# An MLP's seven products with their weight sums made by transfers: two sums leave VectorE for adding DMAs, and three results are summed in DRAM

## The chip, the cores and the metric

The kernel runs on one core of a Trainium2 chip. The metric is the device time of one execution in microseconds, lower is better. Engines are named as the profile names them: PE multiplies matrices, DVE (VectorE) adds and subtracts, ACT (ScalarE) copies and applies functions, POOL (GpSimd) and SP here mainly issue transfers (DMAs), each from a queue of its own that keeps its order.

## The reference, cut to what matters

One inference step of one layer on 384 tokens: 128 of a prompt and 256 of a sample. A projection feeds two mixers (an mLSTM and a pooling mixer), their output is added to the input, and an MLP with 8192 hidden channels follows. Only the MLP is touched by the change:

```python
    h = _rmsnorm(x, norm_w[2]) * (1 + scale_f) + shift_f
    y = jnp.square(jax.nn.relu(h @ w1)) @ w2      # (384 x 2048) @ (2048 x 8192), then @ (8192 x 2048)
    x = x + gate_f * _rmsnorm(y, norm_w[3])
```

All data are float32. The kernel multiplies in a reduced float32 format, with each operand split into a high part (a rounded copy) and a low part (what is left), and three matmuls (high x high, high x low, low x high) for one product.

## The kernel before

The MLP goes by chunks of 1024 hidden channels, that is 8 tiles of 128: `ch` 0 to 7. Hidden tiles are made by groups of w1 (`w1_group`: four slabs of 24 matmuls of 128x384, with the w1 slab loaded by SP, its high part made on ACT at L134 and its low part on DVE at L135). The second product, with w2, is added up over chunks in `y[0..2]`, one tile of 128 tokens by 2048 columns for each token group.

Chunk 0 multiplies by w2 in the plain way. In chunks 1 to 6 (`S_FIRST` to `S_LAST`), for each of the four blocks `n` of 512 columns, and in chunk 7 for n=0 and 1 (`N_LAST` = 2), `mlp_seven` is used: 26 calls, named (ch, n) here. It takes token groups 1 and 2 and even and odd hidden tiles as a 2x2 of blocks, a 2x2 of w2 (row parity r, column half c) as the other, and forms the product with seven block products instead of eight, by sums of blocks. Token group 0 takes its plain products with the same weights on the way. The hidden side of the sums (s1, s2, s4) is made in `evac_pair`, which takes the hidden tiles out of PSUM. The weight side is made here:

- SP loads four blocks of 512 KB: b11 = (0,0), b21 = (1,0), b22 = (1,1), b12 = (0,1). Tiles come from two pools, tag `raw` (3 buffers, shared with the w1 slabs) and tag `raw2` (2 buffers, b21 and b12).
- DVE forms, each into the place of one operand, T1 = b12 - b11 (L1225), T3 = b22 - b12 (L1231), T2 = b22 - T1 (L1235) and T4 = b21 - T2 (L1239).
- Each of the seven weights b11, b21, b22, T1, T3, T2, T4 is split: high part on ACT (L1189), low part on DVE (L1190). The profile calls them hi_b and lo_b for b11, b21 and b22, hi_t and lo_t for the sums.
- PE runs 11 products of 12 matmuls of 128x256 (L1203 to L1205) into five PSUM banks: `x7`, `yz`, `16`, `23`, `45`. The order of use is b11 and b21, then b22, T1, T3, T2, T4.
- The results: DVE adds the bank halves that belong to one output to `y`. R7 (right half of x7) and R1, R6 (bank 16) belong to several outputs; they are summed over the chunks in two SBUF tiles, r7 and r16 (ACT copies in chunk 1, DVE adds at L1212 later). `seven_done` combines them with `y` once, for n=2 and 3 at the end of chunk 6 and for n=0 and 1 in chunk 7 beside its plain products.

The order of the instructions on each engine and in each queue is set when the kernel is built; each engine runs its own in that order. Within a chunk PE runs seven n=0, seven n=1, one w1 group, seven n=2, seven n=3, three w1 groups. So n=1 follows n=0 directly and n=3 follows n=2; with (7,0) and (7,1) these are 13 pairs back to back, in which the second seven's weights must be loaded and summed while the first runs.

Of the kernel before, what the change touches and what calls it, by code (L numbers as in the profile page):

```python
# [43 lines left out]
def hymba_kernel(  # L44
# [1128 lines left out]
    def mlp_seven(ch, n, strp, r16, r7, feeds=()):  # L1173
# [4 lines left out]
        for m, (r, c) in enumerate(((0, 0), (1, 0), (1, 1), (0, 1))):  # L1178
            pool, tag = ((wp, "raw"), (strp, "raw2"))[m % 2]
            raws[r, c] = pool.tile([P, 1024], F32, tag=tag, name=f"w2_{ch}_{n}_{r}{c}", bufs=3 - m % 2)  # L1180
            nc.sync.dma_start(raws[r, c].rearrange("p (j q) -> p j q", q=256),
                              w2v[:, k0 + r:k0 + 8:2, c0 + 256 * c:c0 + 256 * c + 256])
# [42 lines left out]
        tt(b11, b12, b11, op=ALU.subtract)  # L1225
# [1 line left out]
        tt(yx, banks["x7"][:, 0:256].unsqueeze(1).to_broadcast([P, 2, 256]), yx, op=ALU.add)
# [3 lines left out]
        tt(b12, b22, b12, op=ALU.subtract)  # L1231
# [12 lines left out]
        product("45", 0, 1, 2, w)  # L1244
        if first:
            nc.scalar.activation(r7[:, n], banks["x7"][:, 256:], AF.Copy)
            nc.scalar.activation(r16[:, n], banks["16"], AF.Copy)
# [4 lines left out]

    def seven_done(n, r16, r7):

        tt = nc.vector.tensor_tensor
# [8 lines left out]
        tt(y2, y2, v.unsqueeze(1).to_broadcast([P, 2, 256]), op=ALU.add)
# [105 lines left out]
```

## Time and profile before

| | |
|---|---|
| three runs | 1688.34, 1690.98, 1690.77 us (median 1690.77) |
| span of the profiled execution | 1686.4 us |
| PE busy | 1657.3 us (98%), 10965 matmuls |
| DVE busy | 1341.7 us (80%) |
| ACT busy | 752.3 us (45%) |
| POOL busy | 130.9 us (8%) |
| transfers | 320.95 MB, mean 190 GB/s |
| transfers from POOL (software queue q0) | 13.69 MB |

The profiled execution's own time is shown only as its span, from its first to its last instruction; the runs' times, taken without the profiler, contain what lies around it too, and their median is 4.4 us above this span. PE is nearly always busy, at a granted clock near full speed. A line of the profile's groups gives line, engine, operation, tiles and shapes, count, then busy time in us, mean in ns and idle time before; a line of a timeline gives start and length in us. The buffers' numbers are left out of its names, so raw and raw2 tiles of w2 are both `w` there, and the banks are `y_x` (x7), `y_yz` and `y` (the other three).

### The profile page before, as it was taken

To read this page: it belongs to the slowest core of one execution; us is meant where nothing else is said; L and a number is where in the kernel's file an instruction comes from. 1 tells how busy PE (TensorE), PEld (TensorE's weight loads), DVE (VectorE), ACT (ScalarE), POOL (GpSimd) and SP (SyncE) were. 2 spreads that over 40 slices of the span, in tenths; PEclk is the share of its full clock that TensorE was granted. 3 is DMA by queue.
4 is the path that set the end of the run, shared out by engine and by line. 5 is a ranking of instruction groups with operands and counts; after the bars stand their busy time and mean duration, and the time that the engine had idled before them with its cause. 6 is when DMAs were issued, how large, how long until landed. Compare 5 with 4: busy or idle time off the path is not lost.

```text
span 1686.4 us, 27861 instructions
## 1 busy us (share of the span) xinstructions
PE 1657.3 (98%) x10965; PEld 1583.9 (94%) x10965; DVE 1341.7 (80%) x2009; ACT 752.3 (45%) x1225; POOL 130.9 (8%) x181
## 2 busy tenths in 40 slices
PE   6999999999999999999999999999999999999997
PEld 3888999999999989988999999999999999999996
DVE  3677769898998959997797688988588588588688
ACT  4432355555443345543444444444444444444443
POOL 0000002221000023530000000000000000000120
PEclk9999999999999999999999999999999999999999
DMA  9999858776789964754556245544344443443653
GB/s 305 324 297 304 276 153 256 245 248 221 236 265 308 312 206 126 218 153 137 157 169 195 87 138 178 155 150 142 109 150 127 124 139 113 149 125 111 185 184 134
DMA packets 258195, 320.95 MB, mean 190 GB/s; under 512 B 14752, under 2 KB 223248, under 8 KB 257680
## 3 DMA queue, kind: packets, MB, share of 16 engines
q1 hardware_dynamic: 250256, 303.41, 57.1%
q0 software_dynamic: 5856, 13.69, 2.8%
q10 hardware_dynamic: 1952, 2.07, 0.4%
q8 instruction: 86, 1.41, 0.3%
q14 instruction: 45, 0.37, 0.1%
HBM read 308.61 MB, written 10.51 MB: 189 GB/s over the span
## 4 chain that ended last, share of the span: by engine, by line
PE 83%; DVE 9%; DMA 3%; issue 2%; SPq 1%; ACT 1%; POOL 0%; DVEq 0%; ACTq 0%; POOLq 0%
PE acc_w L144 9%; PE acc_w L143 9%; PE acc_w L145 9%; PE v L476 4%; PE y L1204 4%; PE y L1203 4%; PE y L1205 4%; PE u L476 4%; PE acc_wo L143 3%; PE acc_wo L144 3%; PE acc_wo L145 3%; PE y_yz L1203 2%; PE y_yz L1205 2%; PE y_yz L1204 2%; DVE ada_acc L316 2%
## 5 line engine op out<-in xcount | busy, mean ns | idle before, releaser
L144 PE MATMUL acc_w<-h2l,hi_w 128*128 128x384 f32 (+1 forms) x1024 | 346.2, 338 | 0.5 <-DVE h2l L997 0.5
L143 PE MATMUL acc_w<-h2h,hi_w 128*128 128x384 f32 (+1 forms) x1024 | 344.2, 338 | 1.4 <-ACT h2h L993 1.2
L145 PE MATMUL acc_w<-h2h,lo_w 128*128 128x384 f32 (+1 forms) x1024 | 345.1, 337 | 0.0
L135 DVE TENSOR_TENSOR lo_w<-raw_w,hi_w 128x1024 fp32r<-128x1024 f32 x152 | 185.5, 1222 | 134.2 <-ACT hi_w L134 133.7
L134 ACT ACTIVATE hi_w<-raw_w 128x1024 fp32r<-128x1024 f32 x152 | 160.7, 1058 | 211.8 <-PE acc_w L144 95.2
L316 DVE SCALAR_TENSOR_TENSOR ada_acc<-ada_raw,sg,ada_acc 128x1024 f32<-128x1024 f32 (+1 forms) x240 | 252.1, 1082 | 1.9 <-DMA ada_raw<-in_ada_w_dram 1.9
L143 PEld LDWEIGHTS acc_w<-h2h,hi_w 128*128 128x128 f32 x1024 | 192.2, 188 | 3.1 <-ACT h2h L993 2.0
L144 PEld LDWEIGHTS acc_w<-h2l,hi_w 128*128 128x128 f32 x1024 | 192.5, 188 | 1.2 <-DVE h2l L997 0.8
L145 PEld LDWEIGHTS acc_w<-h2h,lo_w 128*128 128x128 f32 x1024 | 192.4, 188 | 0.3 <-DVE lo_w L135 0.2
L1189 ACT ACTIVATE hi_t<-w 128x1024 fp32r<-128x1024 f32 x104 | 109.6, 1060 | 118.6 <-DVE w L1225 33.6
L1190 DVE TENSOR_TENSOR lo_t<-w,hi_t 128x1024 fp32r<-128x1024 f32 x104 | 126.4, 1221 | 15.1 <-ACT hi_t L1189 14.7
L1190 DVE TENSOR_TENSOR lo_b<-w,hi_b 128x1024 fp32r<-128x1024 f32 x78 | 95.3, 1222 | 40.5 <-ACT hi_b L1189 40.4
L1189 ACT ACTIVATE hi_b<-w 128x1024 fp32r<-128x1024 f32 x78 | 82.6, 1060 | 99.2 <-PE acc_w L144 65.9
L134 ACT ACTIVATE hi_wo<-raw_wo 128x1024 fp32r<-128x1024 f32 x32 | 34.0, 1064 | 83.5 <-DMA raw_wo<-in_w_out_dram 65.7
L923 ACT ACTIVATE z<-acc_w 128x384 f32<-128x384 f32 x54 | 26.3, 487 | 75.0 <-PE acc_w L145 75.0
L476 PE MATMUL v<-hi_v,hh 128*128 128x384 f32 (+1 forms) x144 | 47.8, 332 | 0.0
L476 PE MATMUL v<-lo_v,hh 128*128 128x384 f32 (+1 forms) x144 | 46.6, 324 | 0.0
L476 PE MATMUL v<-hi_v,hl 128*128 128x384 f32 (+1 forms) x144 | 46.5, 323 | 0.0
L134 ACT ACTIVATE hi_v<-raw_v 128x768 fp32r<-128x768 f32 (+1 forms) x24 | 18.9, 795 | 60.8 <-DMA raw_v<-in_w_in_dram 40.9
L135 DVE TENSOR_TENSOR lo_wo<-raw_wo,hi_wo 128x1024 fp32r<-128x1024 f32 x32 | 38.8, 1216 | 8.3 <-ACT hi_wo L134 7.5
L143 PE MATMUL acc_k<-hh,hi_k 128*128 128x384 f32 x128 | 44.2, 345 | 0.0
L143 PE MATMUL acc_o<-hh,hi_o 128*128 128x384 f32 x128 | 43.9, 343 | 0.0
(2264 smaller groups left out, 4552.8 us busy)
## 6 DMA issues: line engine op xcount, KB each, us to landing
raw_w<-in_w_dram SPq DMA_DIRECT2D x152, 512.0 KB, 4.3
ada_raw<-in_ada_w_dram SPq DMA_DIRECT2D x130, 512.0 KB, 5.1
w<-in_w_dram SPq DMA_DIRECT2D x104, 512.0 KB, 4.2
raw_wo<-in_w_out_dram SPq DMA_DIRECT2D x32, 512.0 KB, 5.2
u<-in_ada_w_dram SPq DMA_DIRECT2D x18, 512.0 KB, 6.1
raw_u<-in_w_in_dram SPq DMA_DIRECT2D x16, 512.0 KB, 7.1
raw_q<-in_w_in_dram SPq DMA_DIRECT2D x16, 512.0 KB, 4.6
raw_k<-in_w_in_dram SPq DMA_DIRECT2D x16, 512.0 KB, 4.9
```

The lines of the kernel that those rows point to most:

```text
L134: nc.scalar.activation(hi[:, 0:n], raw[:, 0:n], AF.Copy)
L135: low = lambda: nc.vector.tensor_tensor(lo[:, 0:n], raw[:, 0:n], hi[:, 0:n].bitcast(F32), op=ALU.subtract)
L143: nc.tensor.matmul(ps, lh, rh, start=start, stop=False)
L144: nc.tensor.matmul(ps, lh, rl, start=False, stop=False)
L145: mm3.ins = nc.tensor.matmul(ps, ll, rh, start=False, stop=stop).ins
L316: nc.vector.scalar_tensor_tensor(acc[:, g, :], raw[:, a, :], cj, acc[:, g, :], op0=ALU.mult, op1=ALU.add)
L476: nc.tensor.matmul(acc[i][:, 0:n], h[k0 + k][a][:, i * P:(i + 1) * P], (hi, lo)[b][:, k, :], start=k == 0 and a + b == 0, stop=k == nk - 1 ...
L1189: nc.scalar.activation(hi, raw, AF.Copy)
L1190: nc.vector.tensor_tensor(lo, raw, hi.bitcast(F32), op=ALU.subtract)
L1203: nc.tensor.matmul(acc, xh, wh, start=start and j == 0, stop=False)
L1204: nc.tensor.matmul(acc, xh, wl, start=False, stop=False)
L1205: nc.tensor.matmul(acc, xl, wh, start=False, stop=stop and j == 3)
```

## The change

T1 and T3 are no longer made by DVE. Their tile is loaded by SP with block (0,1), and then POOL issues an adding transfer of block (0,0) or (1,1) from DRAM onto it. [...] A seven has five loads and two adding transfers of 512 KB in place of four loads, and b12 has no tile of its own. The tag raw2 has three buffers.

R7, R1 and R6 are no longer summed in SBUF. ACT copies the three into a tile `stage` (128x768, 2 buffers), and POOL stores it to DRAM (`r_dram[n]`) in chunk 1 and adds it there later, 384 KB each. `seven_done` loads the sums back with a POOL transfer. The tiles r7 and r16 (12 KB a partition) are gone.

```diff
--- before.py
+++ after.py
@@ -929,7 +929,7 @@
         a11, a21, a12, a22 = z0[:, P:2 * P], z0[:, 2 * P:], z[:, P:2 * P], z[:, 2 * P:]
         s1, s2, s4 = (s[:, i * P:(i + 1) * P] for i in range(3))
         tt = nc.vector.tensor_tensor
-        tt(s1, a21, a22, op=ALU.add)
+        tt(s1, a21, a22, op=ALU.subtract)
         if t < 8 * S_LAST + 8:
             tt(a21, a11, a21, op=ALU.subtract)
         else:
@@ -941,7 +941,7 @@
             hid["d", t] = hi, lo
         hid[t - 1], hid[t] = split_T(z0, f"hid{t - 1}"), split_T(z, f"hid{t}")
         tt(s2, s1, a11, op=ALU.subtract)
-        tt(s4, a12, s2, op=ALU.subtract)
+        tt(s4, a12, s2, op=ALU.add)
         hid["s", t] = split_T(s, f"hs{t}")
 
     def gate_f():
@@ -1170,17 +1170,21 @@
         for _ in side:
             pass
 
-    def mlp_seven(ch, n, strp, r16, r7, feeds=()):
+    def mlp_seven(ch, n, strp, r_dram, feeds=()):
 
 
         k0, c0, first = 8 * ch, 512 * n, ch == S_FIRST
         raws = {}
-        for m, (r, c) in enumerate(((0, 0), (1, 0), (1, 1), (0, 1))):
-            pool, tag = ((wp, "raw"), (strp, "raw2"))[m % 2]
-            raws[r, c] = pool.tile([P, 1024], F32, tag=tag, name=f"w2_{ch}_{n}_{r}{c}", bufs=3 - m % 2)
-            nc.sync.dma_start(raws[r, c].rearrange("p (j q) -> p j q", q=256),
-                              w2v[:, k0 + r:k0 + 8:2, c0 + 256 * c:c0 + 256 * c + 256])
-        b11, b21, b22, b12 = raws.values()
+        for m, (rc, plus) in enumerate((((0, 0), None), ((1, 0), None), ((0, 1), (0, 0)), ((1, 1), None), ((0, 1), (1, 1)))):
+            pool, tag, nb = (wp, "raw", 3) if m in (0, 3) else (strp, "raw2", 3)
+            t = raws[m] = pool.tile([P, 1024], F32, tag=tag, name=f"w2_{ch}_{n}_{m}", bufs=nb)
+            for q, (r, c) in enumerate((rc,) if plus is None else (rc, plus)):
+                dst, src = t.rearrange("p (j q) -> p j q", q=256), w2v[:, k0 + r:k0 + 8:2, c0 + 256 * c:c0 + 256 * c + 256]
+                if q:
+                    nc.gpsimd.dma_start(dst, src, accum_op=ALU.add)
+                else:
+                    nc.sync.dma_start(dst, src)
+        b11, b21, t1, b22, t3 = raws.values()
         banks = {m: bank(f"y_{ch}_{n}_{m}") for m in ("x7", "yz", "16", "23", "45")}
 
         def split(raw, name):
@@ -1222,46 +1226,47 @@
             product("16", 0, 0, 1, wa, js=js)
             product("yz", 0, 1, 0, wb, js=js)
             product("23", 0, 1, 1, wb, js=js)
-        tt(b11, b12, b11, op=ALU.subtract)
-        yx = ys[0].rearrange("p (a q) -> p a q", a=2)
-        tt(yx, banks["x7"][:, 0:256].unsqueeze(1).to_broadcast([P, 2, 256]), yx, op=ALU.add)
+        tt(ys[0][:, 0:256], banks["x7"][:, 0:256], ys[0][:, 0:256], op=ALU.add)
+        tt(ys[0][:, 256:], ys[0][:, 256:], banks["x7"][:, 0:256], op=ALU.subtract)
         w = split(b22, "b22")
         product("yz", 1, 1, 0, w, stop=False)
         product("23", 1, 2, 2, w)
-        tt(b12, b22, b12, op=ALU.subtract)
-        w = split(b11, "t1")
+        w = split(t1, "t1")
         product("yz", 1, 0, 0, w, start=False)
         product("45", 1, 2, 0, w)
-        tt(b22, b22, b11, op=ALU.subtract)
-        w = split(b12, "t3")
+        tt(b22, b22, t1, op=ALU.add)
+        w = split(t3, "t3")
         product("x7", 1, 0, 2, w)
         add(ys[1], "23")
-        tt(b21, b21, b22, op=ALU.subtract)
+        tt(b21, b21, b22, op=ALU.add)
         w = split(b22, "t2")
         product("16", 1, 2, 1, w)
         add(ys[0], "yz")
         w = split(b21, "t4")
         product("45", 0, 1, 2, w)
+        st = strp.tile([P, 768], F32, tag="stage", name=f"stage_{ch}_{n}", bufs=2)
+        nc.scalar.activation(st[:, 512:], banks["x7"][:, 256:], AF.Copy)
+        nc.scalar.activation(st[:, 0:512], banks["16"], AF.Copy)
         if first:
-            nc.scalar.activation(r7[:, n], banks["x7"][:, 256:], AF.Copy)
-            nc.scalar.activation(r16[:, n], banks["16"], AF.Copy)
+            nc.gpsimd.dma_start(r_dram[n], st)
         else:
-            add(r7[:, n], "x7", 1)
-            add(r16[:, n], "16")
+            nc.gpsimd.dma_start(r_dram[n], st, accum_op=ALU.add)
         add(ys[2], "45")
 
-    def seven_done(n, r16, r7):
+    def seven_done(n, r_dram):
 
         tt = nc.vector.tensor_tensor
         ys = [y[i][:, 512 * n:512 * n + 512] for i in range(3)]
-        r1, r6, v = r16[:, n, 0:256], r16[:, n, 256:], r7[:, n]
+        st = strp.tile([P, 768], F32, tag="stage", name=f"sums_{n}", bufs=2)
+        nc.gpsimd.dma_start(st, r_dram[n])
+        r1, r6, v = st[:, 0:256], st[:, 256:512], st[:, 512:]
         tt(ys[1][:, 0:256], ys[1][:, 0:256], r1, op=ALU.add)
         tt(r6, r6, r1, op=ALU.add)
         tt(v, v, r6, op=ALU.add)
-        tt(r6, r6, ys[2][:, 256:], op=ALU.add)
-        tt(ys[1][:, 256:], ys[1][:, 256:], r6, op=ALU.add)
-        y2 = ys[2].rearrange("p (a q) -> p a q", a=2)
-        tt(y2, y2, v.unsqueeze(1).to_broadcast([P, 2, 256]), op=ALU.add)
+        tt(r6, r6, ys[2][:, 256:], op=ALU.subtract)
+        tt(ys[1][:, 256:], ys[1][:, 256:], r6, op=ALU.subtract)
+        tt(ys[2][:, 0:256], ys[2][:, 0:256], v, op=ALU.add)
+        tt(ys[2][:, 256:], ys[2][:, 256:], v, op=ALU.subtract)
 
     def w1_group(g, feeds=(), n=NTOK):
         gemm_T(w1, [grp(g)], hx2, n, evac_pair, feeds, name="w1")
@@ -1284,25 +1289,25 @@
                 strp = str_scope.enter_context(tc.tile_pool(name="strp", bufs=1, side="right", reuse_waits="tile"))
                 vec.update(pool=strp, acc=strp, slab=512, bufs=3, half=False)
                 ff.rate = RATE_GS
-                r16, r7 = strp.tile([P, 4, 512], F32, name="r16"), strp.tile([P, 4, 256], F32, name="r7")
+                r_dram = [dram.tile([P, 768], F32, name=f"r_dram{n}") for n in range(4)]
             for n in range(4):
-                mlp_seven(ch, n, strp, r16, r7, (ff,))
+                mlp_seven(ch, n, strp, r_dram, (ff,))
                 if n == 1:
                     w1_group(4 * ch + 4, (ff,))
             if ch == S_LAST:
                 ff.finish()
                 for n in range(N_LAST, 4):
-                    seven_done(n, r16, r7)
+                    seven_done(n, r_dram)
             for g in range(1, 4):
                 w1_group(4 * ch + 4 + g, (ff,))
         else:
             load_tail()
             for n in range(N_LAST):
-                mlp_seven(ch, n, strp, r16, r7)
+                mlp_seven(ch, n, strp, r_dram)
 
             def done_late():
                 for n in range(N_LAST):
-                    seven_done(n, r16, r7)
+                    seven_done(n, r_dram)
                     yield
                     for i in range(3):
                         done(i, 512 * n, 512 * n + 512)
```

On DVE, in chunk 3, from the splits of b11 and b21 of seven (3,1) on, the rows were (names are tile, chunk, n and weight; y0 to y2 are the outputs, y_3_0_... and y_3_1_... banks):

```order
L1190 TENSOR_TENSOR lo_3_1_b11_11380<-w2_3_1_00_11366,hi_3_1_b11_11379 128x1024 [waits DMAHW3_49,Activation_49]
L1212 TENSOR_TENSOR r7_8460<-y_3_0_x7_11183,r7_8460 128x256 [waits PE_49]
L1190 TENSOR_TENSOR lo_3_1_b21_11384<-w2_3_1_10_11368,hi_3_1_b21_11383 128x1024 [waits DMAHW5_49,Activation_49]
L1212 TENSOR_TENSOR r16_8459<-y_3_0_16_11185,r16_8459 128x512 [waits PE_49]
L1212 TENSOR_TENSOR y2_4990<-y_3_0_45_11187,y2_4990 128x512 [waits PE_49]
L1225 TENSOR_TENSOR w2_3_1_00_11366<-w2_3_1_01_11372,w2_3_1_00_11366 128x1024 [waits DMAHW7_49,DVE_49]
L1227 TENSOR_TENSOR y0_4988<-y_3_1_x7_11374,y0_4988 128x512 [waits PE_49]
L1190 TENSOR_TENSOR lo_3_1_b22_11442<-w2_3_1_11_11370,hi_3_1_b22_11441 128x1024 [waits DMAHW4_49,Activation_49]
L1231 TENSOR_TENSOR w2_3_1_01_11372<-w2_3_1_11_11370,w2_3_1_01_11372 128x1024 [waits DVE_49]
L1190 TENSOR_TENSOR lo_3_1_t1_11471<-w2_3_1_00_11366,hi_3_1_t1_11470 128x1024 [waits Activation_49]
L1235 TENSOR_TENSOR w2_3_1_11_11370<-w2_3_1_11_11370,w2_3_1_00_11366 128x1024 [waits DVE_49]
L1190 TENSOR_TENSOR lo_3_1_t3_11500<-w2_3_1_01_11372,hi_3_1_t3_11499 128x1024 [waits Activation_49]
```
and with the change they are:

```order
L1194 TENSOR_TENSOR lo_3_1_b11_11431<-w2_3_1_0_11413,hi_3_1_b11_11430 128x1024 [waits DMAHW4_49,Activation_49]
L1194 TENSOR_TENSOR lo_3_1_b21_11435<-w2_3_1_1_11415,hi_3_1_b21_11434 128x1024 [waits DMAHW6_49,PE_49,Activation_49]
L1216 TENSOR_TENSOR y2_4990<-y_3_0_45_11233,y2_4990 128x512 [waits PE_49]
L1194 TENSOR_TENSOR lo_3_1_b22_11493<-w2_3_1_3_11420,hi_3_1_b22_11492 128x1024 [waits DMAHW5_49,Activation_49]
L1229 TENSOR_TENSOR y0_4988<-y_3_1_x7_11425,y0_4988 128x256 [waits PE_49]
L1230 TENSOR_TENSOR y0_4988<-y0_4988,y_3_1_x7_11425 128x256
L1194 TENSOR_TENSOR lo_3_1_t1_11521<-w2_3_1_2_11417,hi_3_1_t1_11520 128x1024 [waits DMASW1_49,Activation_49]
L1237 TENSOR_TENSOR w2_3_1_3_11420<-w2_3_1_3_11420,w2_3_1_2_11417 128x1024 [waits DVE_49]
L1194 TENSOR_TENSOR lo_3_1_t3_11550<-w2_3_1_4_11422,hi_3_1_t3_11549 128x1024 [waits DMASW2_49,Activation_49]
L1241 TENSOR_TENSOR w2_3_1_1_11415<-w2_3_1_1_11415,w2_3_1_3_11420 128x1024 [waits DVE_49]
```
L1225, L1231 and the adds into r7 and r16 are gone; the low parts of T1 and T3 now wait for POOL's transfers (DMASW) in place of DVE.

On SP, the loads of (3,1), which start while (3,0) runs, were in this order:

```order
L1181 DMA w2_3_1_00_11366<-in_w2_dram 128x4x256 [waits DMAHW5_49,DVE_49]
L1181 DMA w2_3_1_11_11370<-in_w2_dram 128x4x256 [waits DMAHW0_49,DVE_49]
L1181 DMA w2_3_1_10_11368<-in_w2_dram 128x4x256 [waits DVE_49]
L128 DMA raw_w1_4096_0_11559<-in_w1_dram 128x4x256 [waits DMAHW6_49,DMAHW2_49,DVE_49]
L1181 DMA w2_3_1_01_11372<-in_w2_dram 128x4x256 [waits DMAHW7_49,DVE_49]
L128 DMA raw_w1_4096_1_11589<-in_w1_dram 128x4x256 [waits DMAHW3_49,DVE_49,Activation_49]
```
and with the change they are:

```order
L1186 DMA w2_3_1_0_11413<-in_w2_dram 128x4x256 [waits DMAHW1_49,DVE_49]
L1186 DMA w2_3_1_3_11420<-in_w2_dram 128x4x256 [waits DMAHW5_49,DMAHW2_49,DVE_49]
L1186 DMA w2_3_1_1_11415<-in_w2_dram 128x4x256 [waits DMASW6_49,DVE_49]
L1186 DMA w2_3_1_2_11417<-in_w2_dram 128x4x256 [waits DMAHW7_49,DMASW7_49,DVE_49]
L128 DMA raw_w1_4096_0_11611<-in_w1_dram 128x4x256 [waits DMAHW3_49,DMAHW0_49,DVE_49]
L1186 DMA w2_3_1_4_11422<-in_w2_dram 128x4x256 [waits DVE_49]
L128 DMA raw_w1_4096_1_11641<-in_w1_dram 128x4x256 [waits DMAHW4_49,DVE_49]
```
w2_3_1_1 is b21, w2_3_1_2 and w2_3_1_4 are block (0,1) for T1 and T3. In the rows before, the two raw2 loads wait for DVE to release the tiles of T3 and T4 of (3,0) (10 and 01). With the change w2_3_1_1 waits for the tile of T1, w2_3_1_2 for that of T3 and w2_3_1_4 for that of T4.

On POOL, between sevens (7,0) and (7,1), the rows were transfers of the residual only:

```order
L1119 DMA x1t2_0_16576<-x1_dram_6367 128x384 [waits DMASW0_49,PE_49]
L1119 DMA x1t2_384_16578<-x1_dram_6367 128x384 [waits DMASW1_49,PE_49]
L1119 DMA x1t2_768_16580<-x1_dram_6367 128x384 [waits DMASW2_49,PE_49]
L1119 DMA x1t2_1152_16582<-x1_dram_6367 128x384 [waits DMASW3_49,DVE_49]
L1119 DMA x1t2_1536_16584<-x1_dram_6367 128x384 [waits DMASW4_49,PE_49,Activation_49]
L1119 DMA x1t2_1920_16586<-x1_dram_6367 128x128 [waits PE_49,DMASW5_49,Activation_49,Pool_49]
```
and with the change they are:

```order
L1119 DMA x1t2_1152_16710<-x1_dram_6367 128x384 [waits DMASW7_49,DVE_49]
L1253 DMA r_dram0_8459<-stage_7_0_16899 128x768 [waits DMASW0_49,Activation_49]
L1184 DMA w2_7_1_2_16908<-in_w2_dram 128x4x256 [waits DMAHW7_49,DMASW1_49]
L1184 DMA w2_7_1_4_16913<-in_w2_dram 128x4x256 [waits DMAHW5_49,DMAHW1_49,DMASW2_49]
L1119 DMA x1t2_1536_16712<-x1_dram_6367 128x384 [waits DMASW3_49,PE_49]
L1119 DMA x1t2_1920_16714<-x1_dram_6367 128x128 [waits DMASW4_49,PE_49,Pool_49]
L1261 DMA sums_0_17119<-r_dram0_8459 128x768 [waits DMASW5_49,DMASW0_49]
```
The store of stage_7_0, which waits for ACT's copies of (7,0)'s last results, stands ahead of the two adding transfers of (7,1).

On DVE, at the end of chunk 6, where `seven_done` for n=2 meets the first w1 group after (6,3):

```order
L1258 TENSOR_TENSOR y1_4989<-y1_4989,r16_8459 128x256
L1262 TENSOR_TENSOR y1_4989<-y1_4989,r16_8459 128x256 [waits DVE_49]
L1264 TENSOR_TENSOR y2_4990<-y2_4990,r7_8460 128x512
L1259 TENSOR_TENSOR r16_8459<-r16_8459 128x256
L135 TENSOR_TENSOR lo_w1_7424_1_16116<-raw_w1_7424_1_16113,hi_w1_7424_1_16115 128x1024 [waits DMAHW4_49,Activation_49]
L1260 TENSOR_TENSOR r7_8460<-r7_8460,r16_8459 128x256 [waits DVE_49]
L135 TENSOR_TENSOR lo_w1_7424_2_16146<-raw_w1_7424_2_16143,hi_w1_7424_2_16145 128x1024 [waits DMAHW6_49,Activation_49]
L1261 TENSOR_TENSOR r16_8459<-r16_8459,y2_4990 128x256 [waits DVE_49]
L135 TENSOR_TENSOR lo_w1_7424_3_16176<-raw_w1_7424_3_16173,hi_w1_7424_3_16175 128x1024 [waits DMAHW0_49,Activation_49]
L1262 TENSOR_TENSOR y1_4989<-y1_4989,r16_8459 128x256 [waits DVE_49]
```
and with the change:

```order
L135 TENSOR_TENSOR lo_w1_7424_0_16214<-raw_w1_7424_0_16211,hi_w1_7424_0_16213 128x1024 [waits DMAHW2_49,Activation_49]
L135 TENSOR_TENSOR lo_w1_7424_1_16244<-raw_w1_7424_1_16241,hi_w1_7424_1_16243 128x1024 [waits DMAHW4_49,PE_49,Activation_49]
L1216 TENSOR_TENSOR y2_4990<-y_6_3_45_16019,y2_4990 128x512 [waits PE_49]
L1263 TENSOR_TENSOR y1_4989<-y1_4989,sums_2_16191 128x256 [waits DMASW0_49]
L1264 TENSOR_TENSOR sums_2_16191<-sums_2_16191 128x256 [waits DMASW6_49]
L135 TENSOR_TENSOR lo_w1_7424_2_16274<-raw_w1_7424_2_16271,hi_w1_7424_2_16273 128x1024 [waits DMAHW7_49,Activation_49]
L1265 TENSOR_TENSOR sums_2_16191<-sums_2_16191 128x256 [waits DVE_49]
L135 TENSOR_TENSOR lo_w1_7424_3_16304<-raw_w1_7424_3_16301,hi_w1_7424_3_16303 128x1024 [waits DMAHW1_49,Activation_49]
L1266 TENSOR_TENSOR sums_2_16191<-sums_2_16191,y2_4990 128x256 [waits DVE_49]
```
L1263, which waits for the sums to be loaded (DMASW0), now stands ahead of the low parts of slabs 2 and 3 of that group.

## The prediction

> **What bounds the kernel now.** I read the page's engine lines and chain first, then PE's waits, then windows over the stage that the change touches (chunks 1 to 7, from about 740 us), and last the timelines of single products.
>
> ```profile
> span 1686.4 us, 27861 instructions
> PE 1657.3 (98%) x10965; PEld 1583.9 (94%) x10965; DVE 1341.7 (80%) x2009; ACT 752.3 (45%) x1225; POOL 130.9 (8%) x181
> PE 83%; DVE 9%; DMA 3%; issue 2%; SPq 1%; ACT 1%; POOL 0%; DVEq 0%; ACTq 0%; POOLq 0%
> ```
> ```profile
> PE y_yz L1204 <- DVE lo_b L1190: 0.4, 1, 0.4
> ```
> ```profile
> 740.00:830.00 90.00, 90.00 (x466) 81.90 (x465) 70.59 (x116) 35.23 (x54) 3.23 (x6) 1.00 0.50 151
> 830.00:1643.10 813.10, 812.59 (x5765) 810.67 (x5764) 634.52 (x783) 372.51 (x469) 18.70 (x31) 1.00 0.47 144
> 1643.10:1686.00 42.90, 33.78 (x170) 28.19 (x168) 34.89 (x75) 14.18 (x30) 1.97 (x3) 0.94 0.39 135
> ```
> The columns of the windows are: us, then PE, PEld, DVE, ACT and POOL busy (with instructions), granted clock, DMA share, GB/s. PE is the bound: between 830 and 1643 us it is idle for 0.5 us of 813, at a granted clock of 1.00, and the one wait of a seven-product in PE's list is 0.4 us on the L1190 split. DVE, which the change relieves, is busy 634.5 of 813 us there, but PE does not wait for it.
>
> Matmuls overlap, so a short lateness hides in the modelled busy time. I look for it in the distance between starts:
> ```profile
> 1116.49 0.28 PE L1203 MATMUL y_yz<-hi_t,hid24h 128*128 128x256 f32 x1
> 1116.61 0.28 PE L1204 MATMUL y_yz<-lo_t,hid24h 128*128 128x256 f32 x1
> ...
> 1119.32 0.28 PE L1203 MATMUL y_x<-hi_t,hid24h 128*128 128x256 f32 x1
> ```
> ```profile
> 899.72 0.28 PE L1203 MATMUL y_yz<-hi_b,hid9h 128*128 128x256 f32 x1
> 900.40 0.39 PE L1204 MATMUL y_yz<-lo_b,hid9h 128*128 128x256 f32 x1 [0.40 <-DVE lo_b L1190]
> ```
> ```profile
> 835.31 0.32 PE L1203 MATMUL y_x<-hi_b,hid14h 128*128 128x256 f32 x1
> ...
> 1295.01 0.36 PE L1203 MATMUL y_yz<-hi_t,hid32h 128*128 128x256 f32 x1
> ```
> The usual pitch is 0.12 us (1116.49 to 1116.61); the longest is 0.68 (899.72 to 900.40). From 830 us on, 22 pitches of 256-column matmuls are long (the first begins with the row of 835.31, the last with that of 1295.01), and their excess sums to 2.8 us, of which about 1.5 us (894 to 911 us) are matmuls waiting for a DVE split. That is all that a faster DVE can give back in this stage: an estimate of 1.5, at most 2.8 us. A seven is 11 products of 12 matmuls, 132 x 0.118 = 15.6 us of PE, and the change leaves these as they are.
>
> **The change, part by part.** DVE's savings first:
> ```profile
> L1225 DVE TENSOR_TENSOR w<-w,w 128x1024 f32<-128x1024 f32 x26 | 31.8, 1221 | 2.2 <-DMA w<-in_w_dram 1.7
> L1231 DVE TENSOR_TENSOR w<-w,w 128x1024 f32<-128x1024 f32 x26 | 31.8, 1221 | 0.4
> L1212 DVE TENSOR_TENSOR r<-y,r 128x512 f32<-128x512 f32 x22 | 15.1, 686 | 0.1
> L1212 DVE TENSOR_TENSOR r<-y_x,r 128x256 f32<-128x256 f32 x22 | 9.2, 418 | 0.0
> L1227 DVE TENSOR_TENSOR y<-y_x,y 128x512 f32<-128x512 f32 x26 | 17.8, 684 | 0.0
> L1247 ACT ACTIVATE r<-y 128x512 f32<-128x512 f32 x4 | 2.4, 599 | 0.3
> ```
> T1 and T3 on DVE go: 31.8 + 31.8 us. The sums into r16 and r7 go: 15.1 + 9.2 us. The one 512-wide add of L1227 becomes two of 256: 2 x 418 - 684 = 152 ns, x26 = +4.0 us, and seven_done turns one 512 add into two, 4 x 0.15 = +0.6 us. DVE's net is -83 us, or about 3 us a seven. It lies beside PE and is worth only the 1.5 us above. ACT gains two copies in each of the 22 later sevens: by the 599 ns row, below 1.2 x 22 = 26 us on an engine busy 372.5 of 813; they sit between two splits of the next seven, and cost PE nothing while those have their margin. The turned signs cost nothing: the same instructions with another operation.
>
> The price that matters is that of the adding transfer. T1 is now usable only when a load has landed and POOL has added a second 512 KB to it, and the load must first find a raw2 buffer. For the second of two sevens back to back (13 pairs: n=0 to 1, n=2 to 3, and the two of chunk 7) the order of SP shows that T1's load waits for the T3 split of the seven before and T3's load for its T4 split. Chunk 3's pair, on DVE's timeline and SP's:
> ```profile
> 1098.63 2.36 DVE L1190 TENSOR_TENSOR lo_t<-w,hi_t 128x1024 fp32r<-128x1024 f32 x2 [0.46 <-ACT hi_t L1189]
> ...
> 1102.20 1.23 DVE L1190 TENSOR_TENSOR lo_t<-w,hi_t 128x1024 fp32r<-128x1024 f32 x1 [0.40 <-ACT hi_t L1189]
> ...
> 1113.61 1.22 DVE L1190 TENSOR_TENSOR lo_t<-w,hi_t 128x1024 fp32r<-128x1024 f32 x1
> ```
> ```profile
> 1099.89 0.37 SPq L1181 DMA_DIRECT2D w<-in_w_dram  x1
> ...
> 1103.45 0.37 SPq L1181 DMA_DIRECT2D w<-in_w_dram  x1
> ```
> ```profile
> w<-in_w_dram SPq DMA_DIRECT2D x104, 512.0 KB, 4.2
> x_dram<-x1b POOLq DMA_DIRECT2D x64, 48.0 KB, 3.6
> x1t<-x_dram POOLq DMA_DIRECT2D x15, 192.0 KB, 4.1
> gf<-gf_dram POOLq DMA_DIRECT2D x10, 192.0 KB, 5.9
> xTr<-xT_dram POOLq DMA_DIRECT2D x16, 192.0 KB, 6.1
> ```
> The first row (two splits, T3 then T2) puts the end of T3's split near 1099.9, just where SP's row issues the load that waits for it; it lands 4.2 us later, at 1104.1. PE starts T1's product at 1116.49, and the splits ahead of it take 1.06 us on ACT (hi, the 104 of L1189) and 1.22 on DVE, so the sum must be there by 1116.49 - 2.3 = 1114.2:
> ```profile
> L1189 ACT ACTIVATE hi_t<-w 128x1024 fp32r<-128x1024 f32 x104 | 109.6, 1060 | 118.6 <-DVE w L1225 33.6
> ```
> The adding transfer may take 1114.2 - 1104.1 = 10.1 us. For T3: issue at 1103.45, landing 1107.7, PE at 1119.32, limit 1117.0, allowed 9.3 us. With n=3 T1 has about 2 us more and T3 the same. Behind a sum that waits on POOL for its load stand only the next sum and the store into r_dram, for which nobody waits but ACT's copy into the same stage tile two sevens later; behind T1's load on SP stands the first slab of the next w1 group, as it stood behind b21's before, so no wait is new there. So the change is hidden while the transfer takes up to about 9.5 us, and each microsecond above is paid once in each pair.
>
> No row of before has an adding transfer. From below: it cannot beat the plain 512 KB of SP, 4.2 us. From above: gf's 5.9 us for 192 KB, all of it scaled by bytes, is 15.7. In between: the POOL rows rise from 3.6 (48 KB) to 4.1 us (192 KB), so a plain 512 KB from POOL is 3.6 + 0.5 x 464/144 = 5.2 us; a sum reads its destination too, and 512 KB at 144/0.47 = 306 GB/s is 1.7 us; gf and xTr, with shorter rows, lie 1.8 to 2.0 us above x1t, of which I take half. 5.2 + 1.7 + 0.9 = 7.8 us, below the limits by 1.5 to 2.3. I take this value as it stands on three rows of the queue that will issue it; the ends 4.2 and 15.7 stay for the range.
>
> [...] No row of before shows an addition. [...]
>
> Two places have less room. At (7,0) to (7,1) POOL's order puts the store of stage_7_0 ahead of the T1 sum of (7,1). The store waits for the copy of bank "16":
> ```profile
> 1626.13 0.28 PE L1203 MATMUL y<-hi_t,hid57h 128*128 128x256 f32 x1
> ...
> 1627.55 0.29 PE L1203 MATMUL y_x<-hi_b,hid56h 128*128 128x256 f32 x1
> ...
> 1636.05 0.29 PE L1203 MATMUL y_yz<-hi_t,hid56h 128*128 128x256 f32 x1
> ```
> ```profile
> 1604.96 6.94 POOL L1119 DMA_DIRECT2D x1t<-x_dram  x12 [1.09 <-PE acc_w L145]
> ```
> The product into "16" ends as the next starts at 1626.13; with ACT's 0.6 us and a POOL issue of about 0.6 to 0.9 us (6.94/12 = 0.58) the sum starts near 1627.6. T1's product comes 8.5 us after (7,1)'s start at 1627.55, at 1636.05; less 2.3 us for the splits and 0.1 for their queue 1633.6. Allowed 6.0 us, so 7.8 is late by 1.8 us (4.2: none; 9.5: 3.5). The second place is seven_done(2) at the end of chunk 6: DVE's order has its add, which waits for the sums_2 load, ahead of the split lo_w of slab 2 of the next w1 group:
> ```profile
> 1565.86 1.22 DVE L135 TENSOR_TENSOR lo_w<-raw_w,hi_w 128x1024 fp32r<-128x1024 f32 x1
> 1568.88 0.69 DVE L1264 TENSOR_TENSOR y<-y,r 128x512 f32<-128x512 f32 x1
> ```
> ```profile
> 1569.96 0.34 PE L143 MATMUL acc_w<-h2h,hi_w 128*128 128x384 f32 x1
> ```
> PE needs that split at 1569.96, so sums_2 must land by 1567.9. On POOL it stands behind the T1 sum of (7,0), whose load waits for a T3 split near 1555.5 to 1557: load landed 1560 to 1561.4, issues about 1 us each, then 4.8 to 6.7 us for 384 KB (3.6 + 0.5 x 336/144 = 4.8, or 1.9 more): 1566 to 1569. Late by 0 to 1.6, taken 0.5 us. POOL itself has room (18.7 us busy of 813), and its 52 sums, 26 stage stores and 4 loads add about 0.9 us each.
>
> The end (1643 to 1686 us, PE 33.8 of 42.9) keeps its work; two loads of sums and two split adds are fed in between products there, and r7's and r16's last adds (1.1 us) leave: taken as zero, -1.1 to +2.
>
> Sum: 1.8 + 0.5 - 1.5 = +0.8 us. The profiled execution was 1686.4 us in its span; the median of the runs, 1690.77, lies 4.4 above it (start, end and the spread of runs), and I keep that difference: 1687.2 + 4.4 = 1691.6 us. Differences below 0.2% (3.4 us) can hardly be told from none here.
>
> **Rivals.** (1) Sums late, slower. If the transfer takes over 9.5 us, every second seven waits: at 9.8 us T3 is 0.5 late in each of 12 pairs, (7,1) 3.8 and chunk 6's end 1: 6 + 3.8 + 1 - 1.5 = +9, 1700 us. At 11 us it is 1.7 x 12 + 5 + 2 - 1.5 = +26, 1717 us. For it: gf's and xTr's 6 us for 192 KB, other loads that share the engines, and that T3's sum stands behind T1's in one queue; against it: the 5.2 us. Its likeliest is 1700.
>
> (2) The DMA engines fill. Added to the stage of 903 us are 26 loads and 52 sums of 512 KB (40.9 MB) and 26 stores of 384 KB (10.2 MB): 51 MB, or 88 if each sum and store counts twice, 57 to 97 GB/s on 144, share 0.47 rising to 0.65 to 0.79. If a row with an addition cost the engines three plain rows, that is 126 MB, 140 GB/s more and a share of 0.93; loads then come late everywhere, 1 to 2.7 us in each of 26 sevens: +26 to +70, about 1735.
>
> (3) Faster: the whole 2.8 us of long pitches and 1.1 us at the end come back and no place is late: 1690.8 - 3.9 = 1686.9 us.
>
> (4) The sums are hidden at both places also: 1690.8 - 1.5 = 1689.3. It belongs to the forecast's own case.
>
> **How the numbers follow.** Hidden but for small waits (1688 to 1694.2): 0.45, since 7.8 is below 9.3, though by less than half the distance between the ends. Sums late (above 1694.2): 0.39. Engines fill: 0.09. Faster: 0.07. So faster 0.07, same 0.45, slower 0.48. The likeliest is 1691.6 with 1688 to 1694.2 for its own range; for 8 in 10 it takes in the late sums up to 1716 (a transfer of 11 us) and the lower case in part: 1687 to 1716.
>
> **What would show it.** Right: PE idle in 830 to 1643 us below 3 us; adding transfers landing in 7 to 9 us; DVE busy about 560 us there; a wait of PE near (7,1)'s T1 product of 1 to 3 us. Wrong: rows of PE waiting for ACT hi_t or DVE lo_t, themselves released by POOL's DMA, in each n=1 seven (transfer above 9.5 us), or a DMA share near 0.9 with longer plain loads than 4.2 us. A transfer below 6 us would leave both places without a wait.

## The result and the profile after

The change made the kernel slower: 1744.91 us (median of four runs, 1739.84 to 1749.37) against 1690.8, a ratio of 1.0322 with a 95% interval of 1.0306 to 1.0339. That is 54 us more, outside the forecast range (1687 to 1716) and on a side to which it had given 0.48. The profiled execution of after was the longest of its four (1749.37 us, span 1747.5) and that of before the shortest (1688.34, span 1686.4), so the two traces account for 61 us.

The head of its page, its DMA queues and the transfers of the change:

```profile
span 1747.5 us, 28113 instructions
PE 1681.5 (96%) x10965; PEld 1597.4 (91%) x10965; DVE 1261.6 (72%) x1943; ACT 762.4 (44%) x1269; POOL 222.4 (13%) x263
q1 hardware_dynamic: 263984, 317.04, 57.7%
q0 software_dynamic: 37120, 52.75, 16.2%
PE 64%; DMA 16%; DVE 12%; issue 4%; ACT 2%; SPq 1%; POOL 1%; DVEq 0%; ACTq 0%; POOLq 0%
...
raw_w<-in_w_dram SPq DMA_DIRECT2D x152, 512.0 KB, 4.7
...
w<-in_w_dram SPq DMA_DIRECT2D x130, 512.0 KB, 4.8
w<-in_w_dram POOLq DMA_DIRECT2D x52, 512.0 KB, 9.5
...
r_dram<-stage POOLq DMA_DIRECT2D x26, 384.0 KB, 9.9
```

DVE is 80.1 us less busy, as intended, and transfers are now 16% of the chain that ended last (3% before). An adding transfer of 512 KB lands 9.5 us after its issue; the line of POOL's issues gives the spread and who waits:

```profile
  ACT hi_t L1193: 95.3, 21
...
DMA to landing us min/median/max: 6.6/9.5/11.4
```

ACT, which makes the high parts of T1 and T3, waits for these transfers 21 times. The waits go on to PE (its list of waits, three of the rows), which had only 0.4 us of them before:

```profile
PE y L1208 <- DVE lo_t L1194: 7.4, 12, 1.3
PE acc_w L145 <- DVE lo_w L135: 6.3, 3, 4.9
PE y_yz L1208 <- DVE lo_t L1194: 5.9, 6, 2.5
```

The same window as in the prediction, and below it two short ones after a pause of PE (granted clock and DMA share are the two numbers ahead of the last):

```profile
830.00:1643.00 813.00, 779.73 (x5370) 767.52 (x5369) 525.27 (x674) 355.07 (x471) 85.84 (x78) 0.99 0.75 191
1620.30:1626.00 5.70, 5.66 (x18) 5.66 (x19) 3.93 (x7) 1.92 (x2) 2.57 (x4) 0.50 0.93 252
1691.00:1698.00 7.00, 6.38 (x28) 6.09 (x29) 6.51 (x7) 3.47 (x4) 0.00 (x0) 0.51 0.16 38
```

PE is idle for 33 of 813 us in place of 0.5. But idle time is not the whole loss: behind a pause the matmuls themselves are slow.

```profile
1614.96 0.34 PE L143 MATMUL acc_w<-h2h,hi_w 128*128 128x384 f32 x1
1615.14 0.34 PE L144 MATMUL acc_w<-h2l,hi_w 128*128 128x384 f32 x1
1620.34 0.69 PE L145 MATMUL acc_w<-h2h,lo_w 128*128 128x384 f32 x1 [4.86 <-DVE lo_w L135]
1620.83 0.52 PE L143 MATMUL acc_w<-h2h,hi_w 128*128 128x384 f32 x1
1621.15 0.52 PE L144 MATMUL acc_w<-h2l,hi_w 128*128 128x384 f32 x1
```

After 4.86 us without work their pitch is 0.32 us (1620.83 to 1621.15) where it was 0.18 ahead of the pause (1614.96 to 1615.14), and the granted clock is 0.50 up to 1626. So this pause of 5 us costs 8.

I took the start of the same matmul in both traces at several places; the difference is the delay so far. Its growth by stage from 830 us on, in us, for after and all experiments (an experiment's name is explained below; "by" gives times of before; the last column is the median of the runs, the others come from the one profiled execution):

| | chunk 1, by 922 | chunks 2 to 6, by 1562 | first w1 groups after, by 1628 | (7,1), by 1643 | all four | run, median us |
|---|---|---|---|---|---|---|
| after | 21.6 | 24.3 | 7.9 | 5.9 | 59.7 | 1744.91 |
| e1 weights only | 18.4 | 16.8 | 0.0 | 3.2 | 38.4 | 1726.28 |
| e2 DRAM sums only | 3.6 | 2.4 | -0.1 | 0.0 | 5.9 | 1696.63 |
| e3 no addition | 15.4 | 1.6 | 1.0 | 4.9 | 22.9 | 1714.44 |
| e4 e1 with 4 buffers | 16.3 | 2.9 | 0.0 | 3.1 | 22.3 | 1713.22 |
| e5 chunk 1 on DVE | 0.5 | 18.6 | 5.5 | 4.7 | 29.3 | 1721.24 |
| e6 sums later | 20.4 | 20.6 | 7.1 | 4.6 | 52.7 | 1744.38 |
| e7 adds at n=0, 2 | 0.6 | -0.4 | -0.1 | 0.0 | 0.1 | 1690.75 |
| e8 repaired | 1.4 | 18.3 | -0.1 | 0.0 | 19.6 | 1715.51 |
| e9 transfers' load only | 16.2 | 13.0 | 0.0 | 0.0 | 29.2 | 1713.86 |
| e10 pairs cured | 0.4 | 2.5 | 0.1 | 0.0 | 3.0 | 1689.44 |

The four stages are not all. Behind (7,1) every kernel with sums in DRAM loses more: 2.5 us in after, 5.6 in e8 and 1.7 to 3.1 in the others. The four without them (e1, e4, e9, e10) lose nothing there.

### The profile page after: what moved, and what is told of

Read it like the earlier page. It is cut to its first block, busy times and chain, and to the rows that moved or that the text cites. A ratio compares the mean times of both kernels' runs of the same rounds, so it can differ in the third digit from the quotient of the medians.

```text
span 1747.5 us, 28113 instructions
## 1 busy us (share of the span) xinstructions
PE 1681.5 (96%) x10965; PEld 1597.4 (91%) x10965; DVE 1261.6 (72%) x1943; ACT 762.4 (44%) x1269; POOL 222.4 (13%) x263
## 3 DMA queue, kind: packets, MB, share of 16 engines
q1 hardware_dynamic: 263984, 317.04, 57.7%
q0 software_dynamic: 37120, 52.75, 16.2%
## 4 chain that ended last, share of the span: by engine, by line
PE 64%; DMA 16%; DVE 12%; issue 4%; ACT 2%; SPq 1%; POOL 1%; DVEq 0%; ACTq 0%; POOLq 0%
DMA w<-in_w_dram 10%; PE acc_w L145 7%; PE acc_w L144 7%; PE acc_w L143 7%; PE v L476 4%; PE u L476 3%; DVE lo_t L1194 3%; PE acc_wo L143 2%; PE acc_wo L144 2%; PE acc_wo L145 2%; DVE ada_acc L316 2%; PE y L1208 2%; PE y L1209 2%; PE y L1207 2%; PE y L1047 1%
## 5 line engine op out<-in xcount | busy, mean ns | idle before, releaser
L1184 POOL DMA_DIRECT2D w<-in_w_dram x52 | 67.2, 1310 | 769.8 <-DMA w<-in_w_dram 420.5
L1019 POOL DMA_DIRECT2D x_dram<-x1b x64 | 39.4, 622 | 45.2 <-DVE x1b L1016 36.7
```

What stands on the lines that cost most here:

```text
L1019: nc.gpsimd.dma_start(x1_blk[:, :, c0:c0 + 32], t[32 * b:32 * b + 32, :].rearrange("p (s c) -> p s c", c=32))
L1184: nc.gpsimd.dma_start(dst, src, accum_op=ALU.add)
```

## The experiments

Theory L: the sums of weights land too late for the second seven of a pair, because the transfers are longer than assumed. Rivals: D, the sums in DRAM are to blame; B, the added transfers fill the DMA engines and delay the other loads; C, chunk 1 is a place of its own.

**e1, the weights' part alone.** In place of the stage tile, `add(r7, "x7", 1)` and `add(r16, "16")` on DVE. All four blocks `n` share one r7 and one r16, so that they fit; what this kernel leaves out is keeping the four sums apart.

> The changed kernel without its DRAM part: T1 and T3 still by a load and an adding transfer, but R1, R6 and R7 are summed by DVE in SBUF as before (the sums of all four blocks go into one tile, so that it fits; the work of each engine is that of before). Theory L (the adding transfers of the weights land too late for the second seven of each pair, 9.5 us where 7.8 was assumed): most of the 54 us stays, less the wait for sums_2 and the slow matmuls behind it (7.8 us) and a shorter wait at (7,1) where no store stands ahead: 1720 to 1732 us. Rival D (the 26 stores into DRAM crowd the queue and the engines): 1690 to 1705. Rival B (all DMA engines are too full): about half, 1715.

Measured: 1726.28 us, ratio 1.0218 (1.0203 to 1.0234), +37 against before on its chip. L's interval held, D's did not. The transfers land in 9.4 us even without the DRAM stores in their queue, and the wait in the w1 group after (6,3) is gone.

**e2, the DRAM part alone.** The kernel before with the change's stage tile, its copies and its `seven_done` (not shown), and

```diff
-            add(r7[:, n], "x7", 1)
-            add(r16[:, n], "16")
+            nc.gpsimd.dma_start(r_dram[n], st, accum_op=ALU.add)
```

> The kernel before with the DRAM part alone: T1 and T3 made by DVE from four loads as before, R1, R6 and R7 copied to a stage tile and summed in DRAM, loaded back by seven_done. Theory L: no wait but that for sums_2 at the end of chunk 6 (up to 5 us, and slow matmuls behind it): 1690 to 1699 us. Rival D: 1710 to 1735. Rival B: about 1700, with plain loads above 4.5 us.

Measured: 1696.63, ratio 1.0046 (1.003 to 1.0061): 7 us. The place was not the one expected: nothing is lost at the end of chunk 6; 3.6 us are in chunk 1, 2.4 in chunks 2 to 6 and 3.1 behind (7,1). 37 and 7 make 44 of 54, so some 10 us appear only with both parts. In the traces, where after is a long run, it is 15 us: 8 in the w1 group after (6,3), 5 in chunks 2 to 6 and nearly 3 at (7,1).

**e3, no addition.**

```diff
-                    nc.gpsimd.dma_start(dst, src, accum_op=ALU.add)
+                    nc.gpsimd.dma_start(dst, src)
```

> The changed kernel with the addition left out of the weight transfers: POOL's second transfer of 512 KB overwrites the tile (T1 and T3 are one block each). Same bytes, same queue, same order. If the addition is what makes the transfer long (packets of 102 ns where the plain ones of SP take 46): landing 6 to 7.5 us instead of 9.5, and of the 54 us at most 20 stay: 1695 to 1712. If POOL's issue (1.3 us) and its start (2 us) are the price: landing 8 to 9.5 and 1725 to 1745.

Measured: 1714.44, ratio 1.0146 (1.013 to 1.0161), two microseconds above the interval for the addition and far below that for the queue. The transfer lands in 6.6 us:

```profile
DMA to landing us min/median/max: 4.5/6.6/9.5
```

So the addition is 2.9 of the 9.5 us, and with it more than half of the loss goes: in chunks 2 to 6 nearly all (24.3 to 1.6 us). At 6.6 us the windows of 9.3 to 10.1 us suffice, as the prediction's limits say. Chunk 1 keeps 15 us without any addition. More than the addition changed, though. POOL's queue carries the same bytes in less than half the packets (37120 in after):

```profile
q0 software_dynamic: 17152, 52.75, 12.0%
```

So the 2.9 us are the price of the addition together with its smaller packets (q0's are 1.4 KB in the mean in after, 3.1 KB in e3); the two are not told apart here.

**e4, one more buffer.** e1 with `(strp, "raw2", 4)`.

> As the first of these (sums of R in one SBUF tile) with four raw2 buffers in place of three, so that in a pair T1's and T3's loads start one split earlier (some 3 us). Theory L (a wait of a few us for each late sum): the pairs' waits nearly go, 1695 to 1708 us. Rival B (engines too full): the transfers get longer by as much as they start earlier, within 4 us of the first of these.

Measured: 1713.22, ratio 1.0148 (1.0129 to 1.0167). This lies between the two intervals, but the table tells them apart by place: in chunks 2 to 6 the loss falls from 16.8 to 2.9 us, though the transfers became no shorter (9.8 us). What stays is chunk 1 (16.3) and (7,1).

**e5, chunk 1 on DVE.** T1 and T3 made by transfers only where `not first`.

> The changed kernel with T1 and T3 of chunk 1's four sevens made by DVE from four loads (signs as in the change), adding transfers from chunk 2 on, DRAM sums kept. Theory C (chunk 1 is a place of its own: the added loads push the loads of the adaLN vector back on SP, DVE waits for them ahead of the last hidden split, and PE restarts slowly): of the 21 us lost by 922 us at most 5 stay, 1725 to 1732 us. Rival (the lateness of the pairs is the whole loss, and chunk 1 only shows it first): 1738 to 1745.

Measured: 1721.24, ratio 1.0188 (1.0169 to 1.0208), 4 us below the interval; chunk 1 loses 0.5 instead of 21.6. Theory C is right on the place. In after's trace the first pause of PE is there:

```profile
838.53 0.58 PE L1207 MATMUL y_x<-hi_b,hid14h 128*128 128x256 f32 x1 [4.54 <-ACT hid14h L193]
```
```profile
829.58 1.41 DVE L316 SCALAR_TENSOR_TENSOR ada_acc<-ada_raw,sg,ada_acc 128x512 f32<-128x512 f32 x2 [4.09 <-DMA ada_raw<-in_ada_w_dram]
```

DVE waits 4.09 us for a load of the adaLN vector's weights, and behind that on DVE stand the sums from which hid14 is split. That load was issued at 819.64, beside the first two adding transfers (819.13 and 821.85, long ones with 10.9 and 11.4 us), and took 9.5 us; the next two took 7.6 and 7.7, where the last three of that row in before took 2.8 to 3.0. Here the transfers do not come late themselves; the loads beside them do: rival B's mechanism, in one place.

This pause and the slow matmuls behind it (granted clock 0.50 from 838.50 to 844.00 us) are 7.5 of the 21.6 us. The other 14 come later in chunk 1, most of them where PE waits for sums that are themselves late, as at T3 of (1,1):

```profile
866.90 0.38 PE L1207 MATMUL y_x<-hi_t,hid8h 128*128 128x256 f32 x1 [2.83 <-ACT hi_t L1193]
```

**e6, seven_done(2) and (3) later,** written after the three w1 groups of chunk 6.

> The changed kernel with seven_done for n=2 and 3 written after the three w1 groups of chunk 6; on DVE its first add then stands behind the split of slab 2 that PE waited 5 us for. If the add that waits for sums_2 is what held PE there: that wait shrinks from 5.0 to about 1 us and the slow matmuls behind it go, 4 to 8 us less: 1736 to 1741. If the split was late for its own load, nothing changes.

Measured: 1744.38, ratio 1.0319 (1.0293 to 1.0344): the time does not change. On DVE the add now stands one w1 slab further back, and the pause only moves on (DVE's row of the first add, after and e6):

```profile
1618.39 0.42 DVE L1263 TENSOR_TENSOR y<-y,sums 128x256 f32<-128x256 f32 x1 [9.90 <-DMA sums<-r_dram]
```
```profile
1617.31 0.43 DVE L1263 TENSOR_TENSOR y<-y,sums 128x256 f32<-128x256 f32 x1 [7.33 <-DMA sums<-r_dram]
```

The first add's place on DVE was not the only cause. In after from 1605 to 1621 us the DMA share is full, sums_2 (384 KB) takes 11.6 us and the w1 slabs of the same moment (512 KB) 8.4 and 12.1, where at that place in before they took 5.2 to 5.8; in e6, with the add one slab further back, ACT waited for the next slab (8.47 us in its row at 1617.20). The rows are after's window, then e6's ACT:

```profile
1605.00:1621.00 16.00, 11.09 (x64) 10.61 (x64) 6.10 (x10) 3.98 (x5) 4.02 (x4) 0.95 1.02 240
```
```profile
1617.20 1.07 ACT L134 ACTIVATE hi_w<-raw_w 128x1024 fp32r<-128x1024 f32 x1 [8.47 <-DMA raw_w<-in_w_dram]
```

**e7, adding transfers only at n=0 and n=2 of chunks 2 to 6,** where a w1 group stands ahead: `adds = not first and n % 2 == 0 and ch <= S_LAST`, all others with `tt(b11, b12, b11, op=ALU.add)` and `tt(b12, b22, b12, op=ALU.add)`, since the change has T1 = b12 + b11 and T3 = b12 + b22, with the signs turned in what uses them; DRAM sums kept.

> Adding transfers only where the seven does not follow another one directly: n=0 and n=2 of chunks 2 to 6 (10 of 26 sevens); all others make T1 and T3 on DVE; DRAM sums kept. Theory L (what costs is the short window of the second of a pair): as with the DRAM sums alone, 1693 to 1701 us. Rival B (each adding transfer costs by its load on the DMA engines): a share 10/26 of the weights' 37 us on top, 1708 to 1714.

Measured: 1690.75, ratio 1.0009 (0.9999 to 1.0018), the time of before and 2 us below L's interval. Its 20 transfers take longer in the median than those of any other run, and nobody waits for them:

```profile
DMA to landing us min/median/max: 9.2/10.3/13.1
```

A long transfer cost nothing where its window is long. Nor did the freed DVE bring anything. And a full DMA share did not cost anything by itself: from 1042 to 1058 us it is 1.10, and PE is busy throughout.

```profile
1042.00:1058.00 16.00, 16.00 (x95) 16.00 (x94) 7.71 (x13) 3.19 (x3) 2.19 (x2) 1.00 1.10 272
```

**e8, the weak places removed together:** T1 and T3 on DVE in chunks 1 and 7, four raw2 buffers, one stage buffer in place of two, seven_done later.

> The change with its weak places removed: T1 and T3 on DVE in chunks 1 and 7, adding transfers in all sevens of chunks 2 to 6, four raw2 buffers (one stage buffer, so that they fit), seven_done of n=2 and 3 later. Theory L with C: little more than the DRAM sums alone, 1696 to 1706 us. Rival B: 1712 or more, with waits of PE in the pairs that the earlier loads don't cure. Faster than before (below 1686) by neither.

Measured: 1715.51, ratio 1.0143 (1.0126 to 1.016). L's interval failed. The time lies in B's, but not with B's sign: the waits in the pairs are gone, and instead each w1 group after n=1 waits for its first slab:

```profile
PE acc_w L143 <- ACT hi_w L134: 7.2, 5, 1.9
```
```profile
996.00:1012.00 16.00, 14.11 (x85) 13.66 (x84) 4.53 (x6) 2.87 (x4) 2.16 (x2) 1.00 1.06 249
```

At the place of the first of them the DMA share is full (1.06). POOL issued two sums and a store with addition there within 4 us (993.38, 996.38 and 997.13), and ACT waited 7.43 us for the load of a w1 slab:

```profile
1010.87 1.06 ACT L134 ACTIVATE hi_w<-raw_w 128x1024 fp32r<-128x1024 f32 x1 [7.43 <-DMA raw_w<-in_w_dram]
```

The plain loads of w2 took 5.1 us in the median of this run, 4.2 in before. Behind (7,1) another 5.6 us are lost, the most of all runs.

**e9, the load alone.** The kernel before, and beside it, into a tile that nothing reads (its main lines; r7 and r16 are shared by the four blocks as in e1):

```diff
+        load = strp.tile([P, 1024], F32, tag="load", name=f"load_{ch}_{n}", bufs=1)
+        for q, (r, c) in enumerate(((0, 1), (0, 0), (1, 1))):
...
+                nc.gpsimd.dma_start(dst, src, accum_op=ALU.add)
```

> The kernel before with the transfers' load alone: T1 and T3 by DVE as before, and beside them, into a tile that nothing reads, 26 plain and 52 adding transfers of 512 KB from POOL, one after the other (R's sums of the four blocks share one tile so that it fits). Nothing waits for them; they only use the queue and the DMA engines. Theory L (the change lost its time because PE waits for the sums themselves): within 4 us of before, 1687 to 1695. Rival B (the adding transfers slow the other loads until PE waits for those): 1700 or more, with PE waiting for splits of w1 or w2 blocks that landed late.

Measured: 1713.86, ratio 1.0136 (1.0118 to 1.0154): against L as I had it, and for B. The transfers were issued close together from 773 to 1345 us, denser than in after, so 24 us is no share of the change's 54; it shows that load alone delays PE when it is dense, 16.2 us of it in chunk 1.

**e10, the pairs cured without DRAM sums.** e4 (with its shared r7 and r16) with T1 and T3 on DVE in chunks 1 and 7.

> Four raw2 buffers and R's sums in one SBUF tile, as in the fourth experiment, and T1 and T3 on DVE in chunks 1 and 7; adding transfers in all 20 sevens of chunks 2 to 6, no transfer of sums. Theory L with C: the loss of that experiment lies almost wholly in chunk 1 (19 us) and at (7,1), so 1692 to 1699. Rival B: 1703 or more, waits for loads inside chunks 2 to 6.

Measured: 1689.44, ratio 0.9998 (0.9989 to 1.0008): the time of before, 3 us below L's interval, with adding transfers in all 20 sevens of chunks 2 to 6. The windows over chunks 2 to 6, for e1, then e10:

```profile
922.00:1540.00 618.00, 610.41 (x4235) 603.67 (x4236) 413.38 (x538) 268.09 (x340) 46.37 (x37) 1.00 0.69 178
```
```profile
922.00:1540.00 618.00, 617.31 (x4327) 614.47 (x4327) 424.76 (x556) 277.31 (x352) 46.33 (x37) 1.00 0.70 181
```

The same load (0.69 and 0.70) and, in e10, even longer transfers (10.0 against 9.4 us) lose 16.8 us with three buffers and 2.5 with four. In these chunks, without the DRAM sums, it is the window and not the amount of load. With the DRAM sums (share 0.73 in after, 0.74 in e8 over the same window) the fourth buffer cures the pairs and the load takes its place. That e8's single stage buffer has no part in this was not tried; in its trace ACT's copies into that buffer (their first line, L1262) wait for PE and DVE only, never for a store:

```profile
its engine sat idle before it (us, times) until:
  PE y_x L1219: 5.8, 17
  DVE ada_acc L316: 0.4, 1
```

## Why the prediction was wrong, point by point

- **What bounds the kernel** held: PE. DVE's relief was sized at -83 us and measured -80.1; it was said to be worth 1.5, at most 2.8 us, and e7 and e10 show no gain outside 0.2%.
- **The limits** (9.3 us for T3, 10.1 for T1) were right in kind and too wide. In chunks 2 to 6, 6.6 us (e3) fit and 9.4 to 9.5 (e1, after) did not. The limits let the adding transfer start as its load lands; in after's trace POOL issues it most often 0.56 us later (landed 1449.39, issued 1449.95), and SP's loads of w2 take 4.8 us in place of 4.2.
- **The price of the adding transfer is the step that failed first:** 7.8 us forecast, 9.5 measured. Its plain part was 6.1 (5.2 + 0.9) and measured 6.6; its addition was 1.7, the author's estimate (that a sum reads its destination is not shown apart by any run), and measured 2.9 (with the smaller packets; 9.5 to 6.6 is a ratio of 1.44). The plain part was carried up to 512 KB from rows of 48 and 192 KB (x_dram, x1t); the DMA share at their places in before was 0.70 (670.6 to 749 us) and 0.91 (1603 to 1615). The least of the 52 took 6.6 us, the longest 11.4. This price alone does not make 54 us: by the prediction's own limits 9.5 us puts T3 0.2 us late in each of 12 pairs and (7,1) 3.5, some 6 us.
- **What a late sum costs** was far too small. Rival 1 priced 9.8 us of transfer at 6 us for the twelve pairs, one wait each; after lost 24.3 us in the ten pairs of chunks 2 to 6. A wait repeats down the chain (T1's lateness, then T3's, then that of T2 and T4, which are made from T1 and split behind T3 on DVE): in PE's waits for low parts at the end of this section, T1's bank `y_yz` has 2.0 us, T3's `y_x` 3.4 and `y`, the banks of T2 and T4, 6.1. One pair of after shows T1's two waits, for the high and for the low part; behind the second the next matmul starts 0.23 us later, where the usual pitch is 0.12:

```profile
1460.55 0.38 PE L1207 MATMUL y_yz<-hi_t,hid40h 128*128 128x256 f32 x1 [0.24 <-ACT hi_t L1193]
1461.81 0.39 PE L1208 MATMUL y_yz<-lo_t,hid40h 128*128 128x256 f32 x1 [0.88 <-DVE lo_t L1194]
1462.04 0.28 PE L1209 MATMUL y_yz<-hi_t,hid40l 128*128 128x256 f32 x1
```

- **Chunk 1 as a place of its own was left out of the sum:** 21.6 us. The prediction looked at windows in steady chunks only, and not at the adaLN loads that share SP, the DMA engines and DVE's order with the first sevens.
- **The end of chunk 6:** 0.5 us forecast, 7.9 measured. The place was right, the landing of sums_2 was not (4.8 to 6.7 us assumed, 11.6 measured), since it ran behind one addition and beside w1 slabs, which were late themselves (e6); the slow clock behind the pause added 2.7.
- **(7,1):** 1.8 forecast, 5.9 measured. The T1 sum landed 8.7 us after its issue at 1681.11, against 6.0 allowed. PE's pause is 2.3 us, another 1.0 follows, and over the 7 us from 1691 on the clock is the 0.51 shown above:

```profile
1688.76 0.27 PE L1209 MATMUL y<-hi_b,hs63l 128*128 128x256 f32 x1
1691.04 0.50 PE L1207 MATMUL y_yz<-hi_t,hid56h 128*128 128x256 f32 x1 [2.01 <-ACT hi_t L1193]
...
1692.93 0.41 PE L1207 MATMUL y_yz<-hi_t,hid58h 128*128 128x256 f32 x1
1693.14 0.41 PE L1208 MATMUL y_yz<-lo_t,hid58h 128*128 128x256 f32 x1
```

- **The end** was taken as zero, at most 2 us: 2.5 in after's trace. What makes it was not followed up.
- **Rival 2** came near the time (1735) and had the share (0.65 to 0.79; measured 0.75), but put the trouble only at 0.93 of a mean. The mean never got there, so its time is near by luck. Loads were late in single stretches of some 16 us, 1.02 and 1.06 at the two places shown; at e7's 1.10 PE was busy for all 16 us.

Not wholly settled: how after's 24.3 us in chunks 2 to 6 divide between late sums and delayed loads. e1, without DRAM sums, has 16.8 there, and e10 shows that all but 2.5 of such a loss is the window's. PE's list of waits in after from 942 to 1606 us, the same chunks, has 11.7 us for the parts of T1 to T4 and 1.4 for w1 slabs; its first four rows:

```profile
PE y L1208 <- DVE lo_t L1194: 6.1, 11, 0.8
PE y_x L1208 <- DVE lo_t L1194: 3.4, 5, 0.9
PE y_yz L1208 <- DVE lo_t L1194: 2.0, 3, 0.9
PE acc_w L145 <- DVE lo_w L135: 1.4, 2, 1.1
```

So nearly all of it is paid at the sums. How much of their lateness comes from plain loads and additions that other transfers had slowed stays open.

## What to carry to other kernels

Work moved from an engine that nobody waits for to a transfer bought nothing here (ratios of 1.0009 in e7 and 0.9998 in e10), and the transfer then has a window: from the release of its buffer to the first use, less the load, the issue and what is made from the sum. Price it with the load of its stage, and ask which loads with a short window land in the fullest stretches; the mean share does not show that (0.75 from 830 to 1643 us in after, 1.02 from 1605 to 1621). Where work must go that way, the remedies that held here are one more buffer (e10, without sums in DRAM) or the places with a long window (e7).
